# Four loads under way instead of two in the weight stream of a mixture of experts

## The chip, the cores and the metric

The kernel runs on one core of a Trainium2 chip. The metric is device time in microseconds, the median of the runs shown; lower is better. All times below are in us unless another unit stands there.

## What is computed

One layer of a hybrid decoder, for 1024 tokens of width 1024. A mixer (a gated linear recurrence and a differential attention, each with a gate, summed and projected) is added to the residual stream. Then comes a mixture of experts: a router picks one of four groups and two of the eight experts in it for every token, and each of the 32 experts does this with its tokens:

```python
def run_block(args):
    tok, w, e = args
    xb = x_pad[tok]
    hid = jax.nn.silu(xb @ w1[e]) * (xb @ w3[e])
    return (hid @ w2[e]) * w[:, None].astype(xb.dtype)

y = lax.map(run_block, ...)
out = jnp.zeros((T + 1, D), xt.dtype).at[buf_tok].add(y.reshape(P, D))
```

`w1` and `w3` are 1024 x 512 and `w2` is 512 x 1024 per expert, in float32: 6 MB per expert, 201 MB in all, each byte of it read once.

## The kernel before

**Stages.** The mixer takes the first part of the span. Then, up to about 912 us, `project` multiplies the merged branches by `w_out`, one tile of 128 tokens after another, and `logits`, `route`, `rank` and `slots` find each token's experts. The rest, from about 920 us, is the loop over the 32 experts, and this is where the change lies.

**The experts' loop.** An expert's tokens (at most 96 per expert in this loop) are gathered by an indirect DMA on GpSimd's queue from the normed tokens in DRAM (`gather`, L1112: `xg<-d_xn,tok_tab`), transposed on TensorE (`turn`, L1122), multiplied by `w1` and `w3` (`hidden`, L1139), turned again (`turn_hidden`, L1156) and multiplied by `w2` (`result`, L1173). `add` weighs the result on ScalarE (L1185, tile `y`) and adds it to the rows of its tokens in DRAM with an accumulating indirect DMA, again on GpSimd's queue (L1186: `out_dram<-y,row_tab`). The second product of an expert comes after the first product of the next one. Every product is made in three passes of float32r operands, so each piece of the weights is first split into a high and a low part: ScalarE copies the high part (`sc.activation`, L1107), VectorE subtracts it for the low part (L1108). TensorE, VectorE and ScalarE run the loop in the order in which it is written.

**The pieces and their buffers.** An expert's weights are six pieces of 128 x 2048 float32 (1 MB). The list `todo` holds the 192 pieces in the order of their use. `fetch` (L849 to L857) takes the next one and loads it on the queue of SyncE (SP), from L851, into the next of 15 raw buffers: nine `early` ones, then in turn with six more. The buffers are old tiles of earlier stages, so the same kind of load has several names in the profile: `spare`, `u`, `mg`, `mh` and `ex`. A raw buffer is free again when its piece has been split. `ahead` (L1098 to L1109) fetches a piece if none is waiting, and splits the oldest fetched one. The parts go to three pairs of buffers (`LEAD = 3`), under names such as `wo`, `u` and `mg`.

**What sets the order of the loads.** Nine pieces are fetched while `project` runs: three in its first step and two after every second tile. The scheduler puts the other 183 loads on SP's queue as early as buffers and waits let it by its own estimate of times. A queue runs in order: a load that waits holds up what stands behind it on SP. A load waits for its buffer, and for one thing more, which `fetch` adds by hand: piece i waits until piece i - 2 has landed. This is the rule that the change touches:

```python
AHEAD = 2
...
if len(loads) >= AHEAD:
    tc.add_manual_dep(ins.ins, loads[-AHEAD].ins.name, WAIT, reason="few loads at once")
```

**What else is on SP's queue there.** `normed` stores each finished tile of tokens twice: the normed tokens to the DRAM scratch `d_xn` (L911), from which the gathers read, and the residual to `out` (L912). The stores of the last tile stand among the loads of pieces 9 to 13 (counted from 0). The first gather needs the last store of `d_xn` and the table of slots `tok_tab` (L1049, VectorE).

Of the kernel before, what the change touches and what calls it, by code (L numbers as in the profile page):

```python
# [20 lines left out]
PSUM = bass.MemoryType.PSUM  # L21
# [9 lines left out]
NE = 32  # L31
# [3 lines left out]
FAR = 2048  # L35
C = 96
AHEAD = 2
LEAD = 3
# [19 lines left out]
def rows(ap, n=128):  # L58
    """A DRAM vector, the same for every partition."""
    return bass.AP(tensor=ap.tensor, offset=ap.offset, ap=[[0, n]] + [list(d) for d in ap.ap])  # L60
# [3 lines left out]
def tile_hybrid(ctx, tc, x, norm_mix, w_in, hg_lb, hg_out_norm, da_q_norm, da_k_norm, da_lambda,  # L64
# [20 lines left out]
    # DRAM scratch  # L85
# [5 lines left out]
    # constants  # L91
# [24 lines left out]
    def rstd_of(ss, n, width, tag):  # L116
        """(ss / n + eps) ** -0.5 per element of [128, width]."""
        r = small.tile([128, width], F32, tag=tag, name=tag)
        ve.tensor_scalar(r, ss, 1.0 / n, EPS, op0=OP.mult, op1=OP.add)  # L119
        gp.tensor_tensor(r, r, nhalf[:, :width], op=OP.pow)  # L120
        return r

    def rstd_of_two(ss):
        """(sum of two mean squares + eps) ** -0.5 per partition."""
        r = small.tile([128, 1], F32, tag="r1", name="r1")
        ve.scalar_tensor_tensor(r, ss[:, 0:1], EPS, ss[:, 1:2], op0=OP.add, op1=OP.add)
        gp.tensor_tensor(r, r, nhalf[:, :1], op=OP.pow)
        return r

    def split(hi, lo, src):  # L130
        """src in two parts whose sum it is."""
        sc.activation(hi, src, AF.Copy)  # L132
        ve.tensor_sub(lo, src, hi.bitcast(F32))  # L133
# [10 lines left out]
    def load_unit(w, segs, kbs=KB, slots=None, staging=staged, later=None):  # L144
        """Columns of a [kbs * 128, n] matrix, in two parts; later: takes what is left to do."""
        parts = [place_for(s_).rearrange("p (k c) -> p k c", k=kbs) for s_ in slots or next(pairs)]
        k = kbs // 2
        for ks in (slice(0, k), slice(k, kbs)):
            raw = staging().rearrange("p (k c) -> p k c", k=k)
            at = 0  # L150
            for c0, n in segs:
                sy.dma_start(raw[:, :, at:at + n], w.rearrange("(k p) c -> p k c", p=128)[:, ks, c0:c0 + n])
                at += n
            if later is None:
                split(parts[0][:, ks], parts[1][:, ks], raw)
            else:
                later.append(lambda ks=ks, raw=raw: split(parts[0][:, ks], parts[1][:, ks], raw))
        return parts

    def passes(ps, lhs, rhs):  # L160
        """ps = the sum of lhs[:, k].T @ rhs[:, k] for operands in two parts each, in three steps."""
        kbs = lhs[0].shape[1]
        for i, (a, b) in enumerate(((0, 0), (0, 1), (1, 0))):
            for k in range(kbs):
                te.matmul(ps, lhs[a][:, k], rhs[b][:, k], start=i == 0 and k == 0, stop=i == 2 and k == kbs - 1)  # L165
            yield
# [5 lines left out]
    # ------------------------------------------------------------------ mixer  # L172
# [4 lines left out]
    def proj_t(t, unit, c0, n):  # L177
        """Tokens t * 128.. of h @ unit[:, c0:c0 + n], tokens on partitions."""
        ps = pmm.tile([128, 512], F32, tag="mm", name="mm")
        hh, hl = hT[t // 4]  # L180
        c = (t % 4) * 128
        three(ps[:, :n], [v[:, :, c:c + 128] for v in (hh, hl)], [v[:, :, c0:c0 + n] for v in unit])
        return ps

    def proj_f(i, unit, c0):
        """Half i of the tokens of h @ unit[:, c0:c0 + 128], columns on partitions."""
        ps = pmm.tile([128, 512], F32, tag="mm", name="mm")
        three(ps, [v[:, :, c0:c0 + 128] for v in unit], hT[i])
        return ps
# [6 lines left out]
    def gate(j, unit):  # L196
        """Gates of both branches, some of the products at a time (12 steps)."""
        for b in range(2):
            for i in range(2):
                ps = pmm.tile([128, 512], F32, tag="mm", name="mm")  # L200
                for n, _ in enumerate(passes(ps, [v[:, :, b * 128:b * 128 + 128] for v in unit], hT[i])):
                    if n < 2:
                        yield
                th = small.tile([128, 512], F32, tag="ostage", name="gth", bufs=2)
                sc.activation(th, ps, AF.Tanh, scale=0.5)
                sy.dma_start(d_gate[j, b, :, i * 512:(i + 1) * 512], th)
                yield

    def step(gen, n=1):
        """The next n steps of something that fills in."""  # L210
        for _ in range(n):
            if next(gen, True):
                return

    # ---- HGRN2
    with ExitStack() as st:
        hg = pool(st, "hgv")
        vh = [hg.tile([128, HG], F32, name=f"vh{t}") for t in range(NT)]
        with ExitStack() as sa:
# [4 lines left out]
            def norm_in(t):  # L224
                """Tokens t * 128.., normed, columns on partitions."""
# [45 lines left out]
        # lower bound of the forget gate, by head  # L271
# [18 lines left out]
        # 1 where a run of 32 tokens starts, 0 elsewhere  # L290
# [15 lines left out]
        for h in range(H):  # L306
            unit = load_unit(win, [(C_HF + h * 128, 128), (C_HQ + h * 128, 128)]) if h else unit0
            f = hg.tile([128, S], F32, name="f")
# [6 lines left out]
            # products of f over runs of 32 tokens; the reference point of a chunk of 64 is the end of its first run  # L315
# [14 lines left out]
            # decay over: 0, 1 pair start to reference; 2, 3 reference to pair end; 4 reference to chunk end (first);  # L330
            # 5 chunk start to reference (second); 6 the pair
# [82 lines left out]
    # ---- differential attention  # L414
# [45 lines left out]
    def rotate(t, unit):  # L460
        """Queries and keys of tokens t * 128..: norm and rotation, each twice."""
# [21 lines left out]
    def columns(t, dup):  # L483
        """The same with columns on partitions: queries as high over low part, keys as both parts twice."""
# [9 lines left out]
    class Softmax:  # L494
        """The two softmaxes of tokens t * 128.., merged but for the first one's sum."""
# [35 lines left out]
        def weigh(self, *ms):  # L531
            """One of them; or, where a bank of PSUM holds one, both."""
# [19 lines left out]
        def attend(self, h, o):  # L552
            """o = the normed sum of the values."""
# [13 lines left out]
    def store(h, t, on):  # L567
        """Four tiles of tokens up to t, columns on partitions, for later."""
# [11 lines left out]
    def keep(t, on):  # L580
        """Two tiles of tokens of the last head up to t, in two parts."""
# [5 lines left out]
    # the gated branches, by 256 tokens: their sum, later its low part; the second branch, later the high part  # L587
    def branch(b, q, jj, unit, oh, ol):
        """256 columns of branch b of tokens q * 256.., gated, onto what is there of the other."""
# [55 lines left out]
    def others(q):  # L645
        """The other heads' part of the second branch."""
# [16 lines left out]
    # what is loaded when: after which tile of tokens, 8 of a head's preparation, then 8 of its attention  # L663
# [4 lines left out]
    # how many steps fill in there  # L668
# [138 lines left out]
    def slot_sums(ps, t, first):  # L807
        """ps [C, 2 * NE] += per slot and expert the token there, less FAR, and its weight, of tokens t * 128..
        whose rank lies in first .. first + C - 1 (first by partition)."""
# [12 lines left out]
    # the experts' weights, in pieces  # L822
# [6 lines left out]
    # an expert's second product comes after the next one's first, for the last but one amid it  # L829
# [19 lines left out]
    def fetch(src=None):  # L849
        raw = place_for(next(raw_slots), F32)  # L850
        ins = sy.dma_start(raw, todo.pop() if src is None else src)  # L851
        if src is None:
            if len(loads) >= AHEAD:
                tc.add_manual_dep(ins.ins, loads[-AHEAD].ins.name, WAIT, reason="few loads at once")
            loads.append(ins)
        fetched.append(raw)

    with fst:
        gmoe = wp.tile([128, D], F32, name="gmoe")
        sc.dma_start(gmoe, rows(norm_moe[0]))  # L860
        # the router's weights times the gains of the norm before it
# [11 lines left out]
        # 0 where a group of a token starts, 1 elsewhere  # L873
# [10 lines left out]
        def project(t, u):  # L884
            """Quarter u of the columns of tokens t * 128.. after the mixer."""
# [47 lines left out]
        def route(t0, t1):  # L933
            """The experts of tokens t0 * 128 .. t1 * 128 - 1 and their weights."""
# [5 lines left out]
            def first(vals, m, run, oh, tag):  # L940
                """Where vals is m, first in its run, as 0 and 1."""
# [24 lines left out]
            # weights: softmax of the two, times the group's  # L966
# [19 lines left out]
        def rank(t0, t1):  # L986
            """How many tokens before each chose its expert."""
# [58 lines left out]
        # where no token is, nothing is fetched, and nothing is added to a row of another token, each its own:  # L1046
        # for expert e the tokens that did not choose it, in order
# [4 lines left out]
    # ------------------------------------------------------------------ experts  # L1052
# [12 lines left out]
    def count():  # L1065
        """For the slots with no token, see above, which of the first tokens goes where; and the rounds beyond the first."""
# [29 lines left out]
    def ahead(src=None):  # L1096
        """The next piece of the weights, in two parts whose sum it is."""
# [17 lines left out]
    def turn(e):  # L1115
        """The tokens of expert e with their columns on partitions."""
# [9 lines left out]
    def hidden(e, xT, again=False, after=(), hold=False):  # L1126
        """after: what follows which piece."""
# [53 lines left out]
    def add(e, yp, row, w):  # L1181
        """The weighed result added to the rows of its tokens."""
# [48 lines left out]
    # experts with more than C tokens: the others, C at a time  # L1231
# [54 lines left out]
```

## Time and profile before

| what | value |
|---|---|
| median of 3 runs | 1591.25 us (1590.67, 1591.25, 1596.08) |
| span of the profiled execution | 1595.7 us |
| its own time beside its span | not printed; of the runs, 1596.08 is the one next above the span, and the median is 4.45 below the span |
| mean granted TensorE clock | 0.979 of full speed |
| busy shares of the span | TensorE 93%, its weight loads 76%, VectorE 65%, ScalarE 48%, GpSimd 15% |
| moved by DMA | 298.03 MB, 187 GB/s as a mean over the span |
| loads of the experts' weights | 192 of 1024 KB |

The span is the time from the first to the last instruction on the core. In the rows of a profile, "PE" is TensorE, "DVE" VectorE, "ACT" ScalarE, "POOL" GpSimd and "SP" SyncE; a "q" behind a name means the engine's sequencer, which issues DMAs and waits. Rows of a timeline give start, length, engine, line, operation, tiles and, in brackets, the idle time ahead of the instruction with what ended it. Rows by window give the window, its length, the busy time of each engine with its count of instructions, the granted clock, the mean busy share of the 16 DMA engines (packets may overlap, so that it can pass 1) and the GB/s moved.

### The profile page before, as it was taken

The numbers are of one execution on the slowest core, as the hardware profiler recorded it, in microseconds if no ns is written. First come the engines' busy times: TensorE is split into PE (matmuls) and PEld (weight loads), VectorE is DVE, ScalarE is ACT, GpSimd is POOL, SyncE is SP. The second block draws the span as 40 slices with busy tenths as digits, with TensorE's granted clock in tenths as the row PEclk, the third lists the DMA queues.
The fourth block names the chain that finished last, engine by engine and source line by source line (L and its number), as shares of the span: only waits on it lengthen the run. The fifth ranks groups of instructions, "written<-read, shape, count | busy, mean of one in ns | idle before, by whom it ended". The sixth has DMA issues, their size and how long they took to land.

```text
span 1595.7 us, 22726 instructions
## 1 busy us (share of the span) xinstructions
PE 1485.4 (93%) x8850; PEld 1213.6 (76%) x8850; DVE 1035.5 (65%) x1642; ACT 767.7 (48%) x1110; POOL 239.5 (15%) x236
## 2 busy tenths in 40 slices
PE   6999999989999999999899879999998999899895
PEld 6988887889888988899899857777755666556563
DVE  6277456247676576774724668888876777677773
ACT  6222222224535244342421347778765666666663
POOL 2000101111111111102600011121111122111102
PEclk9999999999999999999999979999999999999997
DMA  6102121222111121254544689999999999999994
GB/s 224 56 27 64 37 85 35 73 67 60 60 47 54 47 67 61 92 160 151 191 172 162 235 288 323 318 313 317 324 326 301 336 335 326 311 326 342 312 319 128
DMA packets 110740, 298.03 MB, mean 187 GB/s; under 512 B 13328, under 2 KB 68512, under 8 KB 86048
## 3 DMA queue, kind: packets, MB, share of 16 engines
q1 hardware_dynamic: 97968, 273.70, 49.1%
q0 software_dynamic: 7168, 20.98, 6.4%
q10 hardware_dynamic: 5488, 1.81, 0.5%
q8 instruction: 71, 1.16, 0.3%
q14 instruction: 45, 0.37, 0.1%
HBM read 267.63 MB, written 33.03 MB: 188 GB/s over the span
## 4 chain that ended last, share of the span: by engine, by line
PE 48%; issue 25%; DMA 16%; DVE 6%; POOL 3%; ACT 1%; POOLq 0%; SPq 0%; DVEq 0%; ACTq 0%
PE mm L165 35%; DMA out_dram<-y,row_tab 12%; PE mm L557 2%; PE sc L1139 2%; POOL out_dram L1186 2%; DMA th<-d_gate 1%; PE tr L549 1%; PE tr L487 1%; PE sc L508 1%; PE sc L507 1%; DVE f L323 1%; DVE u L133 1%; PE tr L929 1%; POOL xg L1112 1%; DMA st<-in_dram 1%
## 5 line engine op out<-in xcount | busy, mean ns | idle before, releaser
L1139 PE MATMUL sc<-wo,xh 128*96 128x512 f32 x760 | 208.8, 402 | 16.3 <-ACT wo L1107 8.1
L165 PE MATMUL mm<-hh,u 128*128 128x512 f32 x768 | 198.3, 401 | 0.0
L1139 PEld LDWEIGHTS sc<-wo,xh 128*96 128x96 f32 x760 | 117.9, 163 | 89.6 <-DVE wo L1108 26.0
L120 POOL TENSOR_TENSOR r<-r,nhalf 128x1 f32<-128x1 f32 (+1 forms) x103 | 83.4, 810 | 640.9 <-DVE r L119 581.8
L165 PE MATMUL mm<-u,hh 128*128 128x256 f32 x1280 | 169.7, 284 | 10.2 <-ACT hh L132 3.6
L165 PEld LDWEIGHTS mm<-u,hh 128*128 128x128 f32 x1280 | 157.4, 191 | 12.8 <-ACT hh L132 4.6
L165 PEld LDWEIGHTS mm<-hh,u 128*128 128x128 f32 x768 | 140.7, 190 | 27.9
L1108 DVE TENSOR_TENSOR wo<-u,wo 128x2048 fp32r<-128x2048 f32 (+1 forms) x51 | 115.8, 2270 | 46.4 <-ACT wo L1107 46.4
L1107 ACT ACTIVATE wo<-u 128x2048 fp32r<-128x2048 f32 (+1 forms) x52 | 97.8, 1882 | 54.2 <-DMA u<-in_dram 40.2
L1186 POOL DMA_INDIRECT out_dram<-y,row_tab x32 | 68.5, 2140 | 356.0 <-ACT y L1185 342.5
L1108 DVE TENSOR_TENSOR wo<-mh,wo 128x2048 fp32r<-128x2048 f32 x38 | 87.0, 2290 | 35.1 <-ACT wo L1107 35.1
L1139 PE MATMUL sc<-wo,xl 128*96 128x512 f32 x380 | 103.8, 395 | 0.0
L165 PE MATMUL mm<-hl,u 128*128 128x512 f32 x384 | 100.1, 399 | 0.0
L165 PE MATMUL mm<-u,hl 128*128 128x256 f32 x640 | 91.5, 281 | 0.0
L1173 PE MATMUL mm<-wo,hh 128*96 128x512 f32 x264 | 81.1, 411 | 10.6 <-DVE wo L1108 6.1
L1107 ACT ACTIVATE wo<-mh 128x2048 fp32r<-128x2048 f32 x38 | 72.7, 1913 | 32.6 <-DMA mh<-in_dram 23.2
L133 DVE TENSOR_TENSOR u<-st,u 128x1024 fp32r<-128x1024 f32 x52 | 62.2, 1219 | 32.4 <-ACT u L132 23.2
L1139 PEld LDWEIGHTS sc<-wo,xl 128*96 128x96 f32 x380 | 61.6, 162 | 26.7 <-DVE xl L133 0.5
L165 PEld LDWEIGHTS mm<-u,hl 128*128 128x128 f32 x640 | 80.9, 189 | 0.3
L165 PEld LDWEIGHTS mm<-hl,u 128*128 128x128 f32 x384 | 70.1, 189 | 13.9
L1173 PEld LDWEIGHTS mm<-wo,hh 128*96 128x96 f32 x264 | 42.8, 167 | 34.2 <-DVE wo L1108 10.9
L1112 POOL DMA_INDIRECT xg<-d_xn,tok_tab x32 | 38.9, 1216 | 196.2 <-PE tr L1122 173.8
(313 smaller groups left out, 2944.3 us busy)
## 6 DMA issues: line engine op xcount, KB each, us to landing
u<-in_dram SPq DMA_DIRECT2D x63, 1024.0 KB, 7.2
mh<-in_dram SPq DMA_DIRECT2D x51, 1024.0 KB, 6.8
mg<-in_dram SPq DMA_DIRECT2D x40, 1024.0 KB, 7.0
ex<-in_dram SPq DMA_DIRECT2D x24, 1024.0 KB, 7.8
st<-in_dram SPq DMA_DIRECT2D x64, 256.0 KB, 3.9
spare<-in_dram SPq DMA_DIRECT2D x14, 1024.0 KB, 7.2
st<-in_dram SPq DMA_DIRECT2D x20, 512.0 KB, 4.6
d_gate<-gth SPq DMA_DIRECT2D x32, 256.0 KB, 2.1
```

The source lines that it names most:

```text
L120: gp.tensor_tensor(r, r, nhalf[:, :width], op=OP.pow)
L133: ve.tensor_sub(lo, src, hi.bitcast(F32))
L165: te.matmul(ps, lhs[a][:, k], rhs[b][:, k], start=i == 0 and k == 0, stop=i == 2 and k == kbs - 1)
L323: ve.reciprocal(ri, c)
L487: te.transpose(pt[:, g, :], dup[:, g].rearrange("p a b -> p (a b)"), ident)
L557: te.matmul(po[:, :128], self.aT[:, s_, :], vd[s_][:, (h % 2) * 128:(h % 2 + 1) * 128], start=s_ == 0, stop=s_ == self.t)
L1107: sc.activation(hi, r_, AF.Copy)
L1108: (gp if c else ve).tensor_sub(lo, r_, hi.bitcast(F32))
L1112: gp.indirect_dma_start(xgs[e % 2], None, d_xn, bass.IndirectOffsetOnAxis(ap=tok[:, e:e + 1], axis=0), bounds_check=S - 1, oob_is_err=False)
L1139: te.matmul(hp[n], a[:, 4 * g + k], b[:, cs], start=g == 0 and k == 0 and a is xh and b is hi, stop=g == 1 and k == 3 and b is lo)
L1173: te.matmul(yp[n], a[:, 2 * g + k], b[:, cs], start=g == 0 and k == 0 and a is hh and b is hi, stop=g == 1 and k == 1 and b is lo)
L1186: gp.indirect_dma_start(out[0], bass.IndirectOffsetOnAxis(ap=row[:, e:e + 1], axis=0), y, None, bounds_check=S - 1, oob_is_err=True, compu ...
```

## The change

`fetch` chooses the number of loads that may be under way: two for the first nine pieces, as before, and four from the tenth piece on. The diff's core is this; the rest of it removes comments and docstrings, which shifts lines by up to three (the load of L851 is L853 afterwards, the stores of L911 and L912 are L914 and L915) and changes no instruction.

```diff
 AHEAD = 2
+DEEP = 4
+FIRST_LOADS = 9
 LEAD = 3
...
     def fetch(src=None):
         raw = place_for(next(raw_slots), F32)
         ins = sy.dma_start(raw, todo.pop() if src is None else src)
         if src is None:
-            if len(loads) >= AHEAD:
-                tc.add_manual_dep(ins.ins, loads[-AHEAD].ins.name, WAIT, reason="few loads at once")
+            n = AHEAD if len(loads) < FIRST_LOADS else DEEP
+            if len(loads) >= n:
+                tc.add_manual_dep(ins.ins, loads[-n].ins.name, WAIT, reason="few loads at once")
             loads.append(ins)
         fetched.append(raw)
```

The number of buffers, the pieces, their order of use and all work on TensorE, ScalarE and GpSimd stay as they are. The scheduler places some instructions of SP and VectorE elsewhere. On SP's queue, at the end of the projection, this is the order before, from the load of piece 9 (`spare`) on; `out_dram<-x_9553` and the `d_xn` store behind it are those of the last tile of tokens:

```order
L851 DMA spare<-in_dram 128x2048
L851 DMA u_10252<-in_dram 128x2048
L851 DMA mg_10272<-in_dram 128x2048
L851 DMA u_10290<-in_dram 128x2048
L912 DMA out_dram<-x_9553 128x1024
L911 DMA d_xn<-xn 128x1024
L851 DMA mh_10363<-in_dram 128x2048
L851 DMA u_10381<-in_dram 128x2048
L851 DMA u_10399<-in_dram 128x2048
L1234 TENSOR_LOAD rounds
L1234 ISA x2
L851 DMA ex_10438<-in_dram 128x2048
```

And this is the same place after the change:

```order
L853 DMA spare<-in_dram 128x2048
L853 DMA u_10252<-in_dram 128x2048
L853 DMA mh_10363<-in_dram 128x2048
L853 DMA u_10290<-in_dram 128x2048
L853 DMA mg_10272<-in_dram 128x2048
L853 DMA u_10381<-in_dram 128x2048
L915 DMA out_dram<-x_9553 128x1024
L914 DMA d_xn<-xn 128x1024
L853 DMA u_10399<-in_dram 128x2048
L853 DMA ex_10438<-in_dram 128x2048
L853 DMA ex_10458<-in_dram 128x2048
L1237 TENSOR_LOAD rounds
```

The loads into `mh_10363` and `u_10381` (pieces 13 and 14) have moved ahead of the last tile's two stores, and piece 13 ahead of piece 11 (`mg_10272`). Behind this place the loads stand one after another in the order of the pieces, before and after.

On VectorE's queue, at the end of the routing, the table of slots `tok_tab` came before behind the counting of free slots (`nsl`, `over`, `mxn`):

```order
L813 TENSOR_SCALAR rh<-iop,rk_all 128x96
L818 TENSOR_SCALAR tv<-oh_all,wts 128x32
L1071 SCALAR_TENSOR_TENSOR nsl<-ob,nsl 128x32
L1072 TENSOR_SCALAR tokb<-tokn 128x1
L1074 TENSOR_REDUCE mxn<-tr 1x1
L1076 TENSOR_SCALAR over<-over_at,mxn 1x16
L1077 TENSOR_REDUCE mxn<-over 1x1
L1049 TENSOR_SCALAR tok_tab<-sc 96x32
```

After the change it stands ahead of them:

```order
L820 TENSOR_SCALAR tv<-oh_all,wts 128x32
L1052 TENSOR_SCALAR tok_tab<-sc 96x32
L1053 COPY tf<-sc 96x64
L1072 TENSOR_TENSOR nsl<-tr,cum_8587 128x32
L1236 MEMSET first 128x1
L1073 TENSOR_SCALAR nsl<-nsl,tokn 128x32
L1074 SCALAR_TENSOR_TENSOR nsl<-ob,nsl 128x32
L1075 TENSOR_SCALAR tokb<-tokn 128x1
L1077 TENSOR_REDUCE mxn<-tr 1x1
```

The same instructions are there, with the table and the copy behind it (`tf`) ahead of the counting.

## Prediction

> **What bounds the kernel now.** I read the page first: the busy tenths over the span, with the DMA queues.
>
> ```profile
> span 1595.7 us, 22726 instructions
> ...
> PE   6999999989999999999899879999998999899895
> ...
> DMA  6102121222111121254544689999999999999994
> ...
> q0 software_dynamic: 7168, 20.98, 6.4%
> ```
>
> A slice is 39.9 us. From the 25th on, which is the experts' loop, the DMA engines are 0.9 busy or more, so the page alone names two candidates, TensorE (PE) and DMA. Which of them sets the pace is told by the adds of the experts' results, one per expert, in the timeline of GpSimd (POOL).
>
> ```profile
> 985.45 2.22 POOL L1186 DMA_INDIRECT out_dram<-y,row_tab  x1 [7.20 <-ACT y L1185]
> ...
> 1003.39 2.23 POOL L1186 DMA_INDIRECT out_dram<-y,row_tab  x1 [7.21 <-ACT y L1185]
> ...
> 1111.03 2.21 POOL L1186 DMA_INDIRECT out_dram<-y,row_tab  x1 [7.21 <-ACT y L1185]
> ...
> 1170.59 2.22 POOL L1186 DMA_INDIRECT out_dram<-y,row_tab  x1 [12.95 <-ACT y L1185]
> ...
> 1514.79 2.22 POOL L1186 DMA_INDIRECT out_dram<-y,row_tab  x1 [12.84 <-ACT y L1185]
> ...
> 1566.59 1.40 POOL L1186 DMA_INDIRECT out_dram<-y,row_tab  x1 [7.68 <-ACT y L1185]
> ```
>
> From 1003.39 to 1111.03 six experts pass: 17.94 each. From 1170.59 to 1514.79 sixteen pass: 21.5 each. The windows of these two stretches and the waits of the second show why.
>
> ```profile
> 938.60:1130.00 191.40, 191.26 (x923) 138.60 (x922) 166.47 (x113) 150.04 (x129) 31.01 (x21) 1.00 0.95 318
> ...
> 1150.00:1550.00 400.00, 362.60 (x1574) 237.75 (x1573) 292.43 (x187) 262.67 (x224) 64.33 (x36) 0.99 0.96 323
> ```
>
> ```profile
> ACT wo L1107 <- DMA u<-in_dram: 38.2, 25, 3.9
> ```
>
> First TensorE is busy for 191.26 of 191.40 us: 17.94 is its own pace, and it lives on the lead of loaded pieces. Then the lead is spent, ScalarE (ACT) waits for loads (the row is the largest such group), and TensorE is busy for 362.60 of 400. The loads set the pace there, and have run at their own pace all along. The waits of SP's queue from 938.6 to 1565 say what holds a load:
>
> ```profile
> SPq L851 <- DMA u<-in_dram: 170.1, 56, 5.4
> SPq L851 <- DMA mh<-in_dram: 159.6, 47, 5.2
> ...
> SPq L851 <- DVE wo L1108: 16.2, 12, 5.6
> ```
>
> Mostly an earlier load (the rule of two), hardly a buffer. The loads' own times, from SP's timeline and the view of line L851:
>
> ```profile
> 938.62 0.33 SPq L851 DMA_DIRECT2D u<-in_dram  x1
> ...
> 1446.05 0.33 SPq L851 DMA_DIRECT2D mh<-in_dram  x1
> 1448.54 0.33 SPq L851 DMA_DIRECT2D spare<-in_dram  x1
> 1451.11 0.33 SPq L851 DMA_DIRECT2D u<-in_dram  x1
> ...
> 1561.18 0.33 SPq L851 DMA_DIRECT2D mg<-in_dram  x1
> ```
>
> ```profile
> DMA to landing us min/median/max: 4.9/7.2/10.1
> ```
>
> The load at 938.62 is that of piece 18, the one at 1561.18 that of piece 191: 173 gaps of 3.60 us, 21.6 per expert, which is the adds' 21.5. Two under way, each 7.2 us from issue to landing, is one per 3.6: the rule of two and the landing time make the pace together.
>
> **The change: the stream.** The question is whether the 16 DMA engines have room. Short windows of the slow stretch show it.
>
> ```profile
> 1300.00:1302.50 2.50, 2.26 (x10) 1.34 (x10) 1.93 (x3) 2.13 (x2) 1.70 (x1) 1.00 1.01 374
> ...
> 1499.00:1502.50 3.50, 3.50 (x21) 2.74 (x20) 2.09 (x1) 0.14 (x1) 1.01 (x1) 1.00 1.02 425
> ...
> 1509.50:1511.00 1.50, 1.50 (x8) 0.97 (x7) 0.90 (x2) 1.40 (x1) 0.00 (x0) 1.00 0.87 257
> 1511.00:1515.50 4.50, 4.50 (x23) 3.31 (x22) 4.32 (x2) 4.05 (x5) 0.71 (x1) 1.00 0.98 384
> ...
> 1515.50:1517.00 1.50, 1.50 (x8) 1.04 (x7) 0.94 (x3) 1.19 (x1) 1.50 (x1) 1.00 1.05 279
> ...
> 1518.70:1521.50 2.80, 2.80 (x18) 2.18 (x17) 2.34 (x2) 1.91 (x2) 0.00 (x0) 1.00 1.04 230
> ```
>
> ```profile
> 1500.93 1.01 POOL L1112 DMA_INDIRECT xg<-d_xn,tok_tab  x1 [6.48 <-PE tr L1122]
> ```
>
> ```profile
> xg<-d_xn,tok_tab POOLq DMA_INDIRECT x32, 8.1
> ```
>
> ```profile
> 1508.93 0.33 SPq L851 DMA_DIRECT2D u<-in_dram  x1
> ```
>
> While two loads overlap, 374 to 425 GB/s move. At 1508.93 an earlier load has landed and lets its successor be issued; while that one starts, a single load is left, and the rate falls to 257; at 1515.50 it is 279. No gather or add has part in these dips: the gather of 1500.93 lands after some 8.1, at 1509.0, and the add of 1514.79 is being issued for 2.22, until 1517.01. Such dips are what a third and a fourth waiting load fill. At 1518.70 it is 230 for another reason: now that add's rows go through the same engines. That cost stays: q0 (gathers and adds) takes 6.4% of the engines' 1595.7 us, 102 us, or 3.2 per expert.
>
> Bounds. Best: loads land 2.49 and 2.57 apart where nothing disturbs them (1446.05 to 1451.11), so six cost 15.2, and with 3.2 for q0 18.4 per expert. Worst with any gain: only the part fills that the windows show as not busy (0.95 and 0.96), so 3.60 x 0.96 = 3.46 per load, 20.7 per expert. No gain at all, 21.6, is a rival. I take the slowest fed window, 374 GB/s, because I picked these windows for being fed: six loads are 6.29 MB, 16.8 us, with q0's 3.2 it is 20.0 per expert, 3.33 per load. That saves 173 x (3.60 - 3.33) = 46 us (46.7 unrounded; best 92 if TensorE allowed it, worst 25).
>
> What is late next: TensorE at 17.94. The lead of loaded pieces was spent somewhere between 1111.03 and 1170.59, at 6/17.94 - 6/21.6 = 0.057 pieces per us. Now it goes at 6/17.94 - 6/20.0 = 0.034, so it lasts 1.65 times as long from 938.6 on, until 1220 to 1320; the loads set the pace after it, as before. TensorE's own work is what ends the gain. Its floor: from the add at 985.45 (expert 1), expert 30's add comes 29 x 17.94 later, at 1505.7 instead of 1566.59, so the span could end 61 us earlier at most.
>
> **The start of the loop.** SP's order now has two more loads ahead of the last tile's stores. From SP's timeline, the chain of waits and the list of DMA issues:
>
> ```profile
> 908.25 0.33 SPq L851 DMA_DIRECT2D u<-in_dram  x1
> ...
> 911.00 0.33 SPq L911 DMA_DIRECT2D d_xn<-xn  x1
> ...
> 924.10 5.15 SPq L851 DMA_DIRECT2D ex<-in_dram  x2
> ```
>
> ```profile
> 909.65 1.28 DVE xn L910
> ...
> 919.68 0.18 DVE tok_tab L1049
> ...
> 920.79 8.28 DMA xg<-d_xn,tok_tab
> ```
>
> ```profile
> d_xn<-xn SPq DMA_DIRECT2D x8, 512.0 KB, 6.4
> ```
>
> The store's issue isn't later: its data are ready at 910.93 (909.65 + 1.28), and the load of piece 14, now ahead of it, waits for the landing of piece 10, which must be in by 908.25, since that load (piece 12, `u`) waited for it. But its bytes stand behind two more loads. Before, it landed at about 917.4 (911.00 + 6.4), and the gather started at 920.79: 3.4 of cover. Two loads at 2.5 are 5.0, so the gather starts 1.6 later; I take 2. Bounds: 0 (the cover holds) and 10 (the rival below). Behind SP's new waits stand only these stores and loads; the read of `rounds`, moved past two loads, serves the loop after the experts. `tok_tab` moves past five small VectorE instructions, worth nothing, since it needs TensorE's sums just ahead of it.
>
> Between the last load issued then (924.10 + 5.15) and 938.62 SP stood with all buffers full, until the first pieces were split. That remains: the early loads come sooner, but the stream goes on from about 938.6 + 2 as before. So the lead at the start of the loop isn't larger, and the whole gain lies in the 173 gaps.
>
> **Sum.** 1595.7 - 46 + 2 = 1551.7 for the profiled execution. Its own time isn't printed; the median is 4.45 below its span, so the forecast is 1547. For this likeliest case I give 1536 to 1560: fed windows of 384 GB/s instead of 374 give 16.4 + 3.2 = 19.6 per expert, 11 us less, and a little over half the way to the worst bound is 13 more.
>
> **The rivals.**
> First, TensorE becomes the bound. At 425 GB/s an expert costs 14.8 + 3.2 = 18.0, and the stream keeps up with 17.94. Then the floor holds: 1591.25 - 61 + 2 = 1532, and 5 less if the gather's delay vanishes and the tail shrinks by 3. For it: windows at 425. Against: 374 and 384 elsewhere. 0.20.
>
> Second, only idle engine time fills: 3.46 per load, 173 x 0.14 = 25 less and 2 back, 1568. For it: a share of 0.95 to 0.96 leaves no more. Against: in the dip at 1515.50 the share is 1.05 at 279 GB/s, so packets take longer in dips, and the share hides room. 0.22.
>
> Third, two are enough and nothing fills. A load with little beside it takes 4.9, half of which is 2.45, as short as the closest landings; then gathers alone make 3.60, and the result is 1591.25 + 2 = 1593. Against: the dips at 257 and 279, in which no gather ran. 0.08. The Trainium skill, "DMA: Bandwidth & Descriptors", section "Anatomy of one DMA — SWDGE (gpsimd) path", speaks for this rival: it gives a DMA about 2.0 us of fixed cost plus its bytes at 436 GB/s, so an estimate from that page is 4.4 us for 1 MB, whose fixed part a second load covers; by it the sum would be 1593 too. The trace's 4.9 lies near it, but the dips speak against what follows, and that fit is for GpSimd's queue, not SP's.
>
> Fourth, slower: loads under way share the engines evenly instead of coming one after another, and gain nothing. Then the `d_xn` store shares with four loads: 4.7 MB at the 320 GB/s of the loop take 14.7 us instead of 8.2 for two loads, 6.5 more less 3.4 of cover, 3; the gather of 8.28 shares with four loads as well, about 7 more. PE starts 10 later: 1601. It decides only if a load gains under 10/173 = 0.06 us. Against: the loads' spacing of 2.5 shows one landing after another. 0.04.
>
> **How the numbers follow.** The main case has 0.46. A measurement of this kernel can tell about 0.5%, 8 us, from no change. The main case and the first two rivals are faster by more (0.88); of the third most is same, and for what I haven't seen I move 0.03 there: faster 0.85, same 0.11, slower 0.04. The range holds the main case and the first two rivals with a margin: 1526 to 1575.
>
> **What would show it.** Right: the adds 17.94 apart until 1220 to 1320 and about 20 apart after; 340 to 350 GB/s where 323 stood; the median landing of a load near 13 us (4 x 3.33); the dips gone; fewer waits of SP for a load and more for a split (`wo`). If the median landing is 14.4 and the adds stay at 21.5, the third rival is right. The first gather after 920.79 by more than 5 us would refute the start's term. The prediction is wrong if the late adds stay over 21 apart or if the loop's start moves by over 8.

## The result, and the profile after

| kernel | median us (range, runs) | span of the profiled execution |
|---|---|---|
| before | 1593.66 (1590.67 to 1600.02, 4) | 1595.7 |
| after | 1531.53 (1530.54 to 1536.16, 4) | 1534.4 |

The ratio is 0.9604, with a 95% interval of 0.957 to 0.9638: 62 us less. Before now has a fourth run (1600.02), which moves its median from 1591.25 to 1593.66. The profiled execution of the changed kernel is the one of 1536.16 us. One execution of all those below, with eight loads, fell into a slow state (1744.38 us at a mean granted clock of 0.782) and is left out of that kernel's figures.

The page of the changed kernel, in three of the rows that were shown of before:

```profile
span 1534.4 us, 22725 instructions
...
PE   6999999989999999999999986999999999999995
...
DMA  7111211220212012143655466999999999999992
```

The DMA row reads almost as it did, since 0.9 of busy time was there before. What has changed is the row of TensorE: from the 26th slice (a slice is 38.4 us) to the last but one there is only 9. The adds in GpSimd's timeline say the same by experts 1, 2, 29, 30 and 31:

```profile
992.52 2.22 POOL L1189 DMA_INDIRECT out_dram<-y,row_tab  x1 [7.20 <-ACT y L1188]
1010.46 2.23 POOL L1189 DMA_INDIRECT out_dram<-y,row_tab  x1 [7.21 <-ACT y L1188]
...
1494.84 2.19 POOL L1189 DMA_INDIRECT out_dram<-y,row_tab  x1 [15.73 <-ACT y L1188]
1504.44 1.40 POOL L1189 DMA_INDIRECT out_dram<-y,row_tab  x1 [7.42 <-ACT y L1188]
1519.53 1.41 POOL L1189 DMA_INDIRECT out_dram<-y,row_tab  x1 [4.08 <-ACTq L1238]
```

From 992.52 to 1494.84, 28 experts pass, 17.94 us each: TensorE's own pace, now to the end. The windows confirm it (the busy time of TensorE stands behind the window's length, and the last three numbers are granted clock, DMA share and GB/s):

```profile
938.60:1130.00 191.40, 191.26 (x914) 138.34 (x914) 162.85 (x112) 147.69 (x125) 30.07 (x21) 0.99 0.97 350
1130.00:1300.00 170.00, 170.00 (x797) 122.95 (x796) 146.86 (x94) 135.11 (x114) 31.02 (x19) 1.00 1.02 372
1300.00:1500.00 200.00, 200.00 (x937) 144.68 (x936) 173.17 (x112) 158.40 (x134) 33.20 (x20) 1.00 1.00 362
```

The DMA share went from 0.96 to 1.00 or 1.02, but the bytes from 323 to 362 or 372 GB/s. A busy share of 0.96 was not a nearly full resource: a packet that takes longer counts as busy too (a window shown below, with a single load starting, has a share of 0.89 at 139 GB/s).

To see where the 61.3 us between the two spans come from, one more row of before is needed, the add of expert 29:

```profile
1556.72 2.19 POOL L1186 DMA_INDIRECT out_dram<-y,row_tab  x1 [18.50 <-ACT y L1185]
```

From expert 1's add to expert 29's it was 571.27 us and is 502.32: 68.95 less. Up to expert 1's add 7.07 were lost (985.45 to 992.52), and after expert 29's add 0.6 (38.98 to 39.56). -68.95 + 7.07 + 0.6 = -61.3.

How close the loads came to falling behind TensorE is read from SP's waits. First from 938 to 1100, then from 1300 to 1500:

```profile
SPq L853 <- DVE wo L1111: 88.0, 27, 17.9
SPq L853 <- DVE mg L1111: 25.7, 15, 2.7
```

```profile
SPq L853 <- DMA u<-in_dram: 53.3, 20, 3.9
SPq L853 <- DMA mh<-in_dram: 46.9, 16, 4.4
...
SPq L853 <- DVE mg L1111: 0.6, 3, 0.3
```

Until about 1100 a load mostly waits for a split to free its buffer: all buffers are full. Late in the loop it waits for an earlier load, and hardly ever for a buffer. So the stream is still the slower of the two, and lives on the buffers. Its pace, from SP's timeline:

```profile
1083.97 0.33 SPq L853 DMA_DIRECT2D u<-in_dram  x1
...
1488.41 0.33 SPq L853 DMA_DIRECT2D mg<-in_dram  x1
```

The first is the load of piece 63, the second that of piece 191: 128 gaps of 3.16 us, 18.96 per expert, where it was 21.6. Each expert takes 1.02 us from the lead, which lasted until the last piece.

### The profile page after: what moved, and what is told of

It is laid out like the page before. It is cut to its first block, busy times and chain, and to the rows that moved or that the text cites. A ratio compares the mean times of both kernels' runs of the same rounds, so it can differ in the third digit from the quotient of the medians.

```text
span 1534.4 us, 22725 instructions
## 1 busy us (share of the span) xinstructions
PE 1460.5 (95%) x8850; PEld 1222.0 (80%) x8850; DVE 1031.8 (67%) x1642; ACT 769.8 (50%) x1110; POOL 231.5 (15%) x236
## 4 chain that ended last, share of the span: by engine, by line
PE 50%; issue 26%; DMA 11%; DVE 6%; POOL 4%; ACT 1%; POOLq 0%; SPq 0%; ACTq 0%; DVEq 0%
PE mm L167 37%; DMA out_dram<-y,row_tab 8%; POOL out_dram L1189 3%; PE mm L559 2%; PE sc L1142 2%; DMA st<-in_dram 1%; PE tr L551 1%; PE sc L510 1%; DVE u L135 1%; PE sc L509 1%; PE tr L489 1%; DMA th<-d_gate 1%; DVE f L325 1%; PE tr L932 1%; POOL xg L1115 1%
## 5 line engine op out<-in xcount | busy, mean ns | idle before, releaser
L1142 PE MATMUL sc<-wo,xh 128*96 128x512 f32 x760 | 202.4, 395 | 0.1
L167 PEld LDWEIGHTS mm<-u,hh 128*128 128x128 f32 x1280 | 157.2, 191 | 12.1 <-ACT hh L134 4.1
L1142 PEld LDWEIGHTS sc<-wo,xh 128*96 128x96 f32 x760 | 123.2, 162 | 52.9 <-ACT xh L134 0.5
L1176 PE MATMUL mm<-wo,hh 128*96 128x512 f32 x264 | 77.5, 396 | 0.6 <-ACT hh L134 0.6
L1115 POOL DMA_INDIRECT xg<-d_xn,tok_tab x32 | 31.7, 990 | 246.1 <-PE tr L1125 191.3
L134 ACT ACTIVATE u<-st 128x1024 fp32r<-128x1024 f32 x52 | 52.8, 1053 | 30.9 <-PE mm L167 22.1
```

Source lines behind the costliest of these rows:

```text
L1115: gp.indirect_dma_start(xgs[e % 2], None, d_xn, bass.IndirectOffsetOnAxis(ap=tok[:, e:e + 1], axis=0), bounds_check=S - 1, oob_is_err=False)
L1142: te.matmul(hp[n], a[:, 4 * g + k], b[:, cs], start=g == 0 and k == 0 and a is xh and b is hi, stop=g == 1 and k == 3 and b is lo)
L1176: te.matmul(yp[n], a[:, 2 * g + k], b[:, cs], start=g == 0 and k == 0 and a is hh and b is hi, stop=g == 1 and k == 1 and b is lo)
```

## The experiments

The theory to be tested, A: with two loads under way the DMA engines run dry between a landing and the first packets of the load that it lets go; a third and a fourth load fill that gap, until TensorE is the bound. Against it stand a fixed share of the rate for each load (B), crowding of gathers and adds (C), a head start of the early pieces as the whole gain (D), TensorE's work as the bound already before (E), a stream that is well faster once TensorE takes its pieces sooner (F), and gathers and adds as the only cause of the dips (G). All edits are shown against the changed kernel.

### Three and eight under way

```diff
-DEEP = 4
+DEEP = 3
```

> Three loads may be under way from the tenth piece on, instead of four. Theory A (with two, the DMA engines run dry around each landing and the next load's start; every load waiting beside the two fills that gap, and once the stream gives an expert in about 19 us TensorE's 17.94 us sets the pace to the end): two loads are left at a landing, some 5 us of work for the engines, so three are enough: 1531 to 1537 us. Theory B (each load has a fixed share of the rate, so that the rate grows with the number under way): three lie midway between 3.60 and 3.16 us per load, 3.38, or 20.3 us per expert; the lead then ends about expert 10 and the time is 1550 to 1560 us.

Measured: 1531.44 us (1529.03 to 1533.66), 0.9584 of before (0.9529 to 0.964). That is in A's range and far below B's. The view of the loads' line and the adds of experts 27 to 29:

```profile
DMA to landing us min/median/max: 4.9/9.2/11.4
```

```profile
1454.60 2.21 POOL L1189 DMA_INDIRECT out_dram<-y,row_tab  x1 [7.53 <-ACT y L1188]
1473.14 2.21 POOL L1189 DMA_INDIRECT out_dram<-y,row_tab  x1 [16.33 <-ACT y L1188]
1490.15 2.19 POOL L1189 DMA_INDIRECT out_dram<-y,row_tab  x1 [14.81 <-ACT y L1188]
```

9.2 for three is 3.1 per load. The add of expert 28 comes 18.54 after the one before it, but that of expert 29 only 17.01 later, and TensorE is busy for 20.00 of the 20.00 us from 1460 to 1480. So three are just enough here: after 1400 ScalarE waits a few times for a load (2.9 us in all), and TensorE does not.

```diff
-DEEP = 4
+DEEP = 8
```

> Eight loads may be under way from the tenth piece on. Theory A: TensorE is at work without a gap with four already, so eight give 1531 to 1536 us; what can differ is the start, where one more load is queued ahead of the last tile's stores and the first gather comes 0 to 3 us later. The stream's own pace after its lead is gone shows whether four still leave something: below 3.16 us per load if so. Theory C (more loads under way crowd the gathers and the adds, which share the engines): the gathers come later than the transposes that need them, TensorE gets gaps, and the time is above 1540 us.

Measured: 1535.64 us (1534.25 to 1536.74, three runs), 0.9615 of before (0.9544 to 0.9686). That is in A's range. The loop is TensorE's again (expert 1's add to expert 29's: 17.94 each), and C is out. What differs is the start, from SP's and GpSimd's timelines and the chain of waits of this kernel:

```profile
900.30 0.33 SPq L853 DMA_DIRECT2D spare<-in_dram  x1
...
912.27 0.33 SPq L914 DMA_DIRECT2D d_xn<-xn  x1
```

```profile
926.63 1.23 POOL L1115 DMA_INDIRECT xg<-d_xn,tok_tab  x1 [11.61 <-DVE rounds L1081]
```

```profile
912.27 13.32 DMA d_xn<-xn
```

The first gather starts 14.36 us after the issue of the last `d_xn` store. In the kernel before it was 9.79 (911.00 to 920.79), and with four 12.09 (915.01 to 927.10). Four, six and seven loads, from that of piece 9 on, stand ahead of the store in the kernels with two, four and eight. The 2.3 from four to eight is inside the 0 to 3 that was expected. Here the chain has the store's landing, 13.32 us after its issue, and the gather follows it within about 1 us.

### Four from the nineteenth piece on

```diff
-FIRST_LOADS = 9
+FIRST_LOADS = 18
```

> Two loads under way until the eighteenth piece, four from the nineteenth on: the order of loads and stores at the start of the experts' loop is that of the kernel before, only the stream inside the loop has four. Theory A (the gain is made in the loop, by the pace of the stream): 1528 to 1533 us, with the first gather back from 6 to about 4 us behind the kernel before or less, as the d_xn store of the last tile is not behind two more loads. Theory D (the gain comes from pieces 13 to 18 being there sooner, a head start): most of it is lost, 1580 to 1590 us.

Measured: 1527.65 us (1524.28 to 1530.76), 0.9562 of before (0.9505 to 0.9619), by the median 0.35 under A's range. D is out: with the start as it was before, the gain is all there, so it is made inside the loop. The start of this kernel:

```profile
909.74 0.33 SPq L914 DMA_DIRECT2D d_xn<-xn  x1
```

```profile
918.20 0.19 DVE tok_tab L1052
...
919.31 9.35 DMA xg<-d_xn,tok_tab
```

And the same chain of waits in the changed kernel:

```profile
915.01 2.75 DMA d_xn<-xn
917.77 8.40 issue
...
927.10 8.75 DMA xg<-d_xn,tok_tab
```

In the first of these kernels the gather waits for `tok_tab`, as before, and starts 9.57 us after the store's issue. In the changed kernel the chain goes through the store and then 8.40 of "issue", which is the name for time that no record explains (this store's landing has none), and the gather starts 12.09 after the store's issue. That is 2.3 more than before. `tok_tab` was ready at 923.08, three us before GpSimd's queue went on at 926.16, so the gather did not wait for it; that it waited for the store, whose rows stand behind two more loads, is what the kernel with eight shows directly. To see whether the time shows it, the two kernels ran once more side by side.

> The changed kernel as it is, once more, beside the next one on the same chip: 0.957 to 0.964 of the kernel before.

> Two loads under way until the eighteenth piece and four after that, once more, beside the changed kernel. If the start's 2.3 us (the d_xn store of the last tile behind two more loads) are real, it is 2 to 4 us faster than the changed kernel (about 0.998 of it); if the place of the first deep load is worth nothing, the two are equal.

Measured: 1533.73 us (1530.11 to 1534.69) and 1529.44 (1523.89 to 1531.96), 0.9589 (0.9556 to 0.9622) and 0.9564 (0.9533 to 0.9596) of before. By the medians the later change to four was 4 us better both times (the first time not side by side), but the ranges overlap, so that the 2.3 us are not shown in the time. What is sure is the place, since the gather of the changed kernel came 12.1 after the store in this execution too, and that of the other 10.2. By its medians the later change is the fastest of the kernels that leave nothing out.

### The stream by itself: a third of the matmuls left out

To see the stream's own pace TensorE has to be out of its way. The next kernels leave one of the three matmul passes per expert out (so the products lack one of their three terms), and differ in the loads under way: two as in the diff, or four, or eight. Each ran once, as did all kernels after them.

```diff
-DEEP = 4
+DEEP = 2
...
-            for a, b in ((xh, hi), (xl, hi), (xh, lo)):
+            for a, b in ((xh, hi), (xh, lo)):
...
-                for a, b in ((hh, hi), (hl, hi), (hh, lo)):
+                for a, b in ((hh, hi), (hh, lo)):
```

> Two loads under way as in the kernel before, and one of the three matmul passes of each expert left out (the low half of the activations times the high half of the weights): TensorE's work per expert falls from about 17.9 to about 12 us, so that the weights set the pace from the first expert on; gathers, adds and all loads stay. Theory A (the kernel before was bound by its loads after the first quarter): the adds lie about 21.5 us apart through the whole loop and the time is no less than before, 1585 to 1615 us, although a third of the matmuls is gone. Theory E (TensorE's work set the time after all, the loads only followed): the time falls with the work, below 1500 us.

> Four loads under way, and one of the three matmul passes of each expert left out as in the kernel with two that took 1581.75 us: TensorE has some 12 us of work per expert, VectorE some 15, so the stream of the weights alone sets the pace. Theory A (four still have a pace of their own, about 3.16 us per load as seen late in the changed kernel's loop): adds 18.4 to 19.2 us apart and 1520 to 1540 us, so no faster than the changed kernel with all its matmuls. Theory F (the 3.16 us per load there were TensorE's pace passed on through full buffers; the loads alone are well faster): adds 15 to 17 us apart and 1430 to 1480 us.

> As the light kernel with four loads under way, but eight. Theory A (the engines are already full with four, nothing is left to fill): within 0.05 us per load of the kernel with four, 1515 to 1540 us. Theory B (a fixed share of the rate per load): a step as large again as from two to four, 3.48 to 3.16 to about 2.85 us per load, 17.1 us per expert, 1470 to 1490 us.

Measured: 1581.75 us with two, 1518.13 with four, 1519.65 with eight. Windows of the three, in this order:

```profile
1130.00:1300.00 170.00, 122.91 (x481) 73.69 (x480) 125.54 (x80) 112.05 (x96) 28.59 (x16) 0.93 0.96 328
```

```profile
1130.00:1300.00 170.00, 133.69 (x558) 83.45 (x557) 144.82 (x94) 132.86 (x114) 45.82 (x20) 0.96 1.02 370
```

```profile
1130.00:1300.00 170.00, 138.00 (x586) 86.95 (x584) 149.22 (x99) 135.52 (x117) 71.50 (x20) 0.97 1.02 377
```

With two, a third less work on TensorE moves the time from 1597.65 (before, beside this run) to 1581.75 only: E is out, the kernel before was bound by its loads, which move 328 GB/s here and 323 with all matmuls. (1581.75 is 3 us under A's range: from 984.24 to 1080.58 six experts ran on the lead at 16 us each, which I had not counted, and the adds from 1104.50 to 1543.22 lie 20.9 apart.) With four it is 370 GB/s, not more than with all matmuls (372), and the adds lie 18.7 apart from 1182.03 to 1462.37: the 3.16 us per load were the stream's own pace, and F is out. 1518.13 is 2 us under A's range, but the kernel before took only 1582.53 beside it, in one run; as shares of before the two are 0.9593 and 0.9604 for the changed kernel, so a third less work on TensorE gains next to nothing. TensorE and the stream are nearly level in the changed kernel. With eight it is 377, and no less time: B is out, and next to nothing is left to fill.

### The stream without gathers and adds

Three light kernels more leave out the gathers from the fourth expert on and the adds of experts 2 to 30 as well (those rows are neither fetched nor added), and have one, two or four loads under way (`DEEP` at 1, 2 or 4).

```diff
+        if 1 < e < NE - 1:
+            return
         gp.indirect_dma_start(out[0], bass.IndirectOffsetOnAxis(ap=row[:, e:e + 1], axis=0), y, None,
...
-                if e + 3 < NE:
+                if e + 3 < 3:
                     gather(e + 3, tok_tab)
```

> Two loads under way, the light matmuls, and the gathers from the fourth expert on and the adds of the experts 2 to 30 left out (their rows are not fetched and not added), so that the loads have the DMA engines to themselves. Theory A (the gap around a landing is the loads' own): it stays, the mean rate is about 350 GB/s instead of 405, 2.95 to 3.1 us per load, 17.7 to 18.6 us per expert, 1490 to 1520 us. Theory G (two loads are enough by themselves, and only the gathers and adds in between make the engines run dry): 2.6 us per load, 15.2 to 15.8 us per expert where VectorE's splits bound it, 1420 to 1445 us.

> As the one before, light and without those gathers and adds, but with four loads under way. Theory A: the gap is filled, 2.55 to 2.7 us per load, down to VectorE's 15.2 us per expert: 1420 to 1450 us, 60 us below the kernel with two. Theory G: the same as with two, within 10 us.

> As the light kernels without the gathers from the fourth expert on and the adds of the experts 2 to 30 (and without the third matmul pass), from the tenth piece on with only one load under way. It shows how long a load takes by itself. Theory A (each load has a fixed time of some 2.5 us, from its issue to its first packet and from its last packet to the next issue, in which it moves nothing): 2.53 us as with four, and those 2.5, is 5.0 us per load, 30 us per expert; 1800 to 1900 us. Theory G (a load beside no other has little dead time, about 0.5 us): 3.0 us per load, 18 us per expert, about 1510 us.

Measured: 1509.52 us with two, 1442.81 with four (before beside these: 1582.53), 1844.77 with one (before: 1598.27). Windows of the kernels with one, two and four:

```profile
1130.00:1300.00 170.00, 115.12 (x339) 62.51 (x339) 90.85 (x59) 80.28 (x67) 0.00 (x0) 0.77 0.63 212
```

```profile
1130.00:1300.00 170.00, 130.76 (x499) 78.69 (x498) 130.26 (x84) 119.02 (x102) 0.00 (x0) 0.91 0.84 309
1300.00:1400.00 100.00, 82.81 (x367) 53.13 (x366) 94.61 (x62) 85.17 (x73) 0.00 (x0) 1.00 0.98 385
```

```profile
1130.00:1300.00 170.00, 149.65 (x673) 98.22 (x671) 170.00 (x113) 155.30 (x136) 0.00 (x0) 1.00 1.01 415
```

With four, VectorE is busy for 170.00 of 170.00, so its splits are the bound, and the stream gives at least 415 GB/s, 2.53 us per load. With two, and nothing else on the engines, it is 309 in the first window: G is out, the gap is the loads' own. The kernel with one load shows its size, in SP's timeline, the view of the loads' line, and three windows of one period:

```profile
1106.51 0.33 SPq L853 DMA_DIRECT2D u<-in_dram  x1
1111.58 0.33 SPq L853 DMA_DIRECT2D mh<-in_dram  x1
```

```profile
DMA to landing us min/median/max: 4.7/4.9/7.7
```

```profile
1110.75:1112.50 1.75, 1.16 (x4) 0.56 (x4) 0.04 (x1) 0.90 (x1) 0.00 (x0) 1.00 0.03 9
1112.50:1113.50 1.00, 0.00 (x0) 0.00 (x0) 0.00 (x0) 1.00 (x2) 0.00 (x0) 1.00 0.89 139
1113.50:1115.75 2.25, 1.16 (x4) 0.56 (x4) 2.20 (x1) 1.54 (x4) 0.00 (x0) 0.92 0.93 390
```

A load alone takes 4.9 from issue to landing, and the next one is issued 5.1 us after it here. For 1.75 us next to nothing moves, for another 1.00 only 139 GB/s, and then the bulk of the load in 2.25. At 415 GB/s its bytes would need 2.53, so about half of a load's period, some 2.5 us, is lost. A second load covers 2.53 us of that at most, which is just the gap itself, so that two are on the edge. The two windows of the kernel with two show both sides of it, and SP's timeline how they differ:

```profile
1062.86 0.33 SPq L853 DMA_DIRECT2D spare<-in_dram  x1
1065.35 0.33 SPq L853 DMA_DIRECT2D u<-in_dram  x1
1069.57 0.33 SPq L853 DMA_DIRECT2D mg<-in_dram  x1
1072.01 0.33 SPq L853 DMA_DIRECT2D u<-in_dram  x1
...
1350.80 0.33 SPq L853 DMA_DIRECT2D mh<-in_dram  x1
1353.36 0.33 SPq L853 DMA_DIRECT2D spare<-in_dram  x1
1356.09 0.33 SPq L853 DMA_DIRECT2D u<-in_dram  x1
```

```profile
1069.50:1071.50 2.00, 0.81 (x4) 0.29 (x3) 2.00 (x2) 1.90 (x2) 0.00 (x0) 1.00 0.54 119
```

At first the gaps between issues are 2.5 and 4.2 in turn: loads run in pairs, and after a pair the engines are nearly dry (119 GB/s in the window just shown). In the later rows they are 2.5 to 2.7, and 385 GB/s move in that stretch, with the same rule of two. What put them into step isn't in the records.

### Half-size loads

```diff
+        v = todo.pop() if src is None else src
+        for c in (0, 1024):
+            ins = sy.dma_start(raw[:, c:c + 1024], v[:, c:c + 1024])
+            if src is None:
+                if len(loads) >= 4:
+                    tc.add_manual_dep(ins.ins, loads[-4].ins.name, WAIT, reason="few loads at once")
+                loads.append(ins)
```

This stands in place of the load in `fetch`, on the light kernel without those gathers and adds.

> The same light kernel without those gathers and adds, each 1 MB piece loaded as two loads of 0.5 MB (128x1024) with four of these under way from the fifth on: as many loads at once as in the changed kernel, as many bytes as in the kernel before. Theory A (what counts is the bytes still queued while one load's fixed time passes): as with two whole loads, 3.0 to 3.4 us per piece, 1490 to 1540 us. Theory B (what counts is the number of loads): as with four whole ones, below 2.75 us per piece, 1440 to 1460 us.

Measured: 1444.07 us. This is B's number; what I had expected by A is wrong. A window and SP's waits from 1000 to 1400:

```profile
1130.00:1300.00 170.00, 149.54 (x672) 98.24 (x671) 170.00 (x115) 155.27 (x135) 0.00 (x0) 1.00 1.01 386
```

```profile
SPq L855 <- DMA u<-in_dram: 94.9, 98, 1.7
...
SPq L855 <- DVE wo L1112: 2.6, 9, 0.4
```

VectorE is full here too, so the time alone would say little; but a load waits for loads and hardly for a buffer, so 386 GB/s is what four halves give by themselves, where two wholes with the same bytes gave 309 (and 385 only in the stretch without pairs). I had counted the bytes under way. What has to cover a landing is what the other loads still hold: one whole piece of two (2.53 us of work), three halves of four (3.8 us), two wholes of three (5.1 us), against about 2.5 of gap. That fits all the runs, but it was fitted after this one, and no later run tests it.

## Why the prediction was right, and where it was not

The forecast was 1547 with 1526 to 1575; the time is 1531.53. The sign, the place and the mechanism held: loads set the pace of the kernel before (light kernel with two), the dips are the loads' own (no gathers, still 309 GB/s), and more loads under way fill them. But the outcome is that of the first rival, 1532, to which I gave 0.20, and not of the main case. That its number fits within 1 us is partly luck: its floor was 8 us too cautious, and the start cost 7 us in the profiled execution where it had 2.

**The step that failed is the fed rate.** The prediction took "the slowest fed window, 374 GB/s" for the loads' 6.29 MB and added 3.2 us for q0, which made 20.0 per expert. Measured is 18.96. The view of the DMA queues in the changed kernel, from 1083.97 to 1488.41 (the 128 gaps), splits this by queue: q1 has the loads, q0 the gathers and adds, and the last two columns are MB and the time of their packets as a share of the engines' time.

```profile
q1 hardware_dynamic: 18514, 134.84, 85.8%
q0 software_dynamic: 4928, 14.60, 15.9%
```

85.8% of 404.44 us for 128 loads is 16.3 us per expert, where 374 GB/s had given 16.8: the loads moved at 389 GB/s while they had the engines, and the window of 384 was nearer. In the same way q0 took 3.0, close to the 3.2 of the prediction. And the shares add up to more than 1, so the two overlap by some 0.3 us per expert, where the prediction put them end to end. These are the 0.5, 0.2 and 0.3 from 20.0 to 18.96. The window of 374 (before, 1300.00 to 1302.50) held loads alone, so that adding q0 to it was right. GpSimd issues an add in it, but the view of the window's queues has no q0:

```profile
q1 hardware_dynamic: 130, 0.93, 100.5%
```

It was one short window, the slowest of three, and stood for the whole loop.

**The lead.** The formula was right and its answer wrong with that rate. At 18.96 the lead goes at 6/17.94 - 6/18.96 = 0.018 pieces per us instead of 0.057, so it lasts 3.15 times as long as the 172 to 232 us of before: until 1480 to 1670, where the last load is issued at 1488.41. No stretch at 20 per expert came. With 18.96 in it, the same formula gives the first rival's outcome. That rival named 425 GB/s and 18.0 for its condition; it needed neither, since a stream that is 1 us per expert too slow is carried by the buffers.

**TensorE's floor.** "61 us earlier at most" was 8 us short: it placed expert 30's add a whole 17.94 after expert 29's, but the last two experts' work is interleaved, and that add comes 9.6 later (1494.84 to 1504.44; before 1556.72 to 1566.59). The term itself measured 68.95.

**The start.** Predicted 2, measured 2.3 from the change. The other 4 of the 6.3 by which the first gather came later were there before any moved instruction (the `spare` load at 903.04 for 899.03), and not in the second execution of the same kernel, where it is at 897.31. As argued, the store's issue was no later (11.97 us after that load in both); its bytes were. The move of `tok_tab` was worth nothing: it was ready 3 us before the gather could start, and the store came last.

**The other rivals.** "Only idle engine time fills" (1568) failed, and for the reason given against it: the share hides room. "Slower" (1601) needed 7 us more for the gather itself; it took 8.75 for 8.28. "Two are enough" (1593) failed as a forecast, but it had something: in one stretch two loads did reach 385 GB/s. Its rule from the Trainium skill, "DMA: Bandwidth & Descriptors", section "Anatomy of one DMA — SWDGE (gpsimd) path", gives a fixed cost of about 2.0 us besides the bytes; the load alone, on SP's queue, has about 2.4 (4.9 less 2.53). That is near what the page gives for GpSimd's queue, but that a second load covers it follows only where the loads keep out of step.

**What was to show it.** The median landing with four, forecast near 13 us, was 11.8 in the changed kernel's second execution. 340 to 350 GB/s were forecast and 362 to 372 came. SP's waits moved from loads to splits early in the loop, not late.

## What to carry to other kernels

A rule of "so many transfers at once" is judged by what the others still hold when one lands, against the time from a landing to the next one's first bytes; measure that time with one transfer under way. In these runs others that held about as much (one whole load) were on the edge, and others that held half as much again (three halves) were nearly enough. Take the rate of a stream, and the time of the queues beside it, from the view by queue over a long stretch, not from one short window. And a producer may be slower than its consumer if the buffers last to the end: multiply the deficit by the count before calling it the bound.

## What the runs showed of the hardware that was not expected

- A DMA share of 0.96 moved 323 GB/s, one of 1.02 372, and one of 1.01 without gathers 415. The share says little about what is left: where a single load starts, 0.89 moved 139.
- Two 1 MB loads under way gave 309 GB/s for 170 us and 385 for the next 100, in one execution, with the same rule.
- Loads of 0.5 MB (4 KB per partition) gave 386 to 395 GB/s with four under way, where whole ones gave at least 415.
- Where TensorE was often idle its granted clock was lower: 0.77 in the window with one load (115.12 busy of 170), 0.91 with two (130.76), 1.00 with four (149.65). Its busy time alone does not set it: with two loads beside gathers and adds the clock was 0.93 at 122.91.
